# Layer norm with gelu, bound by DMA: 2 MB transfers of 16 KB runs, and the result written over the input's buffer

## Chip, cores, metric

One core of a Trainium2 chip. The metric is the device time of one execution in microseconds (us), median of several. "The profile" is the page and the views made from the trace of one profiled execution, whose span leaves out about 1.8 us of the measured time.

## The reference

```python
mean = np.mean(x, axis=-1, keepdims=True)          # x: 8 x 1024 x 2048 float32
var = np.var(x, axis=-1, keepdims=True)
out = gamma * (x - mean) / np.sqrt(var + eps) + beta
return 0.5 * out * (1 + np.tanh(np.sqrt(2 / np.pi) * (out + 0.044715 * out ** 3)))
```

It reads 67.1 MB and writes 67.1 MB.

## The kernel before

The 8192 rows are cut into 64 tiles of 128 rows, one row of 8 KB per partition. A tile is loaded (1 MB). DVE takes its statistics, ACT normalises it to bf16, DVE multiplies by gamma, and TensorE adds beta into PSUM. ACT then applies gelu from PSUM into an output buffer, which is stored (1 MB). Loads and stores are all issued by SP in one order.

```python
xin  = ctx.enter_context(tc.tile_pool(name="xin", bufs=AHEAD + 2))    # 12 buffers of 8 KB a partition
outs = ctx.enter_context(tc.tile_pool(name="outs", bufs=6))           # 6 buffers of 8 KB a partition
# gamma once and beta twice: 8 KB rows into single partitions, issued from ACT
def load(i):
    xt = xin.tile([P, d], f32, tag="xt")
    o(nc.sync.dma_start(out=xt, in_=xf[i * P:(i + 1) * P]))
def gelu(i):
    ot = outs.tile([P, d], f32, tag="ot")
    o(nc.scalar.activation(out=ot, in_=pss.pop(i), func=ACT.Gelu_apprx_tanh))
    o(nc.sync.dma_start(out=of[i * P:(i + 1) * P], in_=ot))
for t in range(T + 2):
    if t + AHEAD < T: load(t + AHEAD)          # AHEAD = 10
    if t < T: stats(t)
    if 0 <= t - 1 < T: norm(t - 1)
    if 0 <= t - 2 < T: gelu(t - 2)
    if 0 <= t - 1 < T: beta_mm(t - 1); scale(t - 1)
# ... (statistics, normalising and matmuls cut)
```

## Time and profile before

| what | value | how to read it |
|---|---|---|
| time | 325.39 us (325.36 to 325.52) | median |
| span of the profiled execution | 323.5 us | |
| DMA queue's share of 16 engines | 98.7% | the bound |
| busiest compute engine | ACT, 78% | has room |
| plateau | 426 GB/s from 36 to 310 us | |
| from 310 us to the end | 306 GB/s over 11.5 us | the only long stretch under the plateau |

The slices of the span, the stretches and the waits stand in the prediction.

### The profile page before, as it was taken

To read this page: it belongs to the slowest core of one execution; us is meant where nothing else is said; L and a number is where in the kernel's file an instruction comes from. 1 tells how busy PE (TensorE), PEld (TensorE's weight loads), DVE (VectorE), ACT (ScalarE), POOL (GpSimd) and SP (SyncE) were. 2 spreads that over 40 slices of the span, in tenths; PEclk is the share of its full clock that TensorE was granted. 3 is DMA by queue.
4 is the path that set the end of the run, shared out by engine and by line. 5 is a ranking of instruction groups with operands and counts; after the bars stand their busy time and mean duration, and the time that the engine had idled before them with its cause. 6 is when DMAs were issued, how large, how long until landed. Compare 5 with 4: busy or idle time off the path is not lost.

```text
span 323.5 us, 2348 instructions
## 1 busy us (share of the span) xinstructions
PE 239.9 (74%) x510; PEld 62.1 (19%) x520; DVE 249.9 (77%) x386; ACT 253.2 (78%) x132; POOL 123.7 (38%) x201
## 2 busy tenths in 40 slices
PE   5588888887776876866866867767768677686880
PEld 2122222222111111111211211111112111121220
DVE  3799999998787787787787887877877868778940
ACT  3779999987787877877877877878778777788982
POOL 1143444444435334344344244353353432524420
DMA  7999999999999999999999999999999999999976
GB/s 293 428 423 421 402 424 425 424 426 428 425 427 427 425 425 428 424 429 426 425 428 425 426 427 427 427 424 426 427 425 428 423 428 427 423 428 425 426 312 264
DMA packets 18452, 134.40 MB, mean 415 GB/s; under 512 B 2051, under 2 KB 2051, under 8 KB 2051
## 3 DMA queue, kind: packets, MB, share of 16 engines
q1 hardware_dynamic: 18432, 134.23, 98.7%
q8 instruction: 4, 0.07, 0.1%
q14 instruction: 10, 0.08, 0.1%
q10 hardware_dynamic: 6, 0.02, 0.0%
HBM read 67.13 MB, written 67.11 MB: 415 GB/s over the span
## 4 chain that ended last, share of the span: by engine, by line
issue 52%; POOL 37%; ACT 3%; DVE 3%; DMA 2%; another core or an unknown queue 0%; POOLq 0%; ACTq 0%
POOL nm L103 20%; POOL rs L101 11%; POOL ve L98 6%; DMA b_row<-in_beta_dram 2%; DVE st L94 2%; ACT ot L130 1%; DVE b_hl L139 1%; ACT yk L110 1%; ACT b_hi L81 1%; ACT b_hl L80 1%; DVE zg L122 0%; POOLq L101 0%; DVE mv L96 0%; ACT L46 0%
## 5 line engine op out<-in xcount | busy, mean ns | idle before, releaser
L126 PE MATMUL ps<-zg,ident 128*128 128x512 bf16 x246 | 116.1, 620 | 68.1 <-DVE zg L122 63.9
L94 DVE BATCH_NORM_STATS2 st<-xt 128x6 f32<-128x512 f32 x256 | 157.7, 678 | 4.2 <-DMA xt<-in_x_dram 4.2
L130 ACT ACTIVATE ot<-ps 128x2048 f32<-128x2048 f32 x64 | 119.9, 1873 | 51.2 <-DMA out_dram<-ot 49.8
L110 ACT ACTIVATE yk<-xt,nm,rs 128x2048 bf16<-128x2048 f32 x64 | 133.4, 2084 | 8.0 <-POOL nm L103 8.0
L117 PE MATMUL ps<-b_hl,ones_b 33*128 33x512 bf16 x256 | 120.5, 624 | 4.2 <-DVE b_hl L139 2.1
L122 DVE TENSOR_TENSOR zg<-yk,g_t 128x2048 bf16<-128x2048 bf16 x64 | 78.0, 1218 | 51.2 <-ACT yk L110 51.2
L98 POOL TENSOR_SCALAR ve<-mv 128x1 f32<-128x1 f32 x64 | 19.8, 309 | 175.0 <-DVE mv L96 175.0
L103 POOL TENSOR_SCALAR nm<-mv,rs 128x1 f32<-128x1 f32 x64 | 66.8, 1044 | 6.3
L126 PEld LDWEIGHTS <-ident 128*128 128x128 bf16 x256 | 32.4, 127 | 153.9 <-issue 153.1
L117 PEld LDWEIGHTS <-ones_b 33*128 33x128 bf16 x256 | 27.1, 127 | 92.6 <-issue 91.1
L101 POOL TENSOR_TENSOR rs<-ve,mhalf 128x1 f32<-128x1 f32 x64 | 36.1, 564 | 5.3
L96 DVE BATCH_NORM_AGGREGATE mv<-st 128x2 f32<-128x24 f32 x64 | 16.9, 264 | 6.3
L86 PE MATMUL g_ps<-g_row,ones 1*128 1x512 f32 x8 | 7.2, 1072 | 3.7 <-DMA g_row<-in_gamma_dram 3.7
L80 ACT ACTIVATE b_hl<-b_row 1x2048 bf16<-1x2048 f32 x1 | 1.9, 1908 | 4.8 <-DMA b_row<-in_beta_dram 4.8
L86 PEld LDWEIGHTS g_ps<-g_row,ones 1*128 1x128 f32 x8 | 2.5, 325 | 6.8 <-issue 6.8
L139 DVE TENSOR_TENSOR b_hl<-b_row,b_hi 1x2048 bf16<-1x2048 f32 x1 | 2.3, 2280 | 1.8 <-ACT b_hi L81 1.8
L88 ACT ACTIVATE g_t<-g_ps 128x2048 bf16<-128x2048 f32 x1 | 1.9, 1877 | 0.3 <-PE g_ps L86 0.3
L81 ACT ACTIVATE b_hi<-b_row 1x2048 bf16<-1x2048 f32 x1 | 1.9, 1908 | 0.0
L46 ACT ACT_TABLE_LOAD x1 | 1.3, 1283 | 0.7 <-PEq L163 0.7
L78 DVE MEMSET b_hl<- 33x1024 uint32 x1 | 0.9, 912 | 1.0 <-PEq L163 1.0
L73 POOL TENSOR_SCALAR_AFFINE_SELECT ident<-ident 128x128 bf16<-128x128 bf16 x1 | 0.3, 293 | 0.1
L66 POOL MEMSET ones<- 1x128 f32 x1 | 0.2, 194 | 0.3 <-POOLq L163 0.3
(7 smaller groups left out, 0.9 us busy)
## 6 DMA issues: line engine op xcount, KB each, us to landing
xt<-in_x_dram SPq DMA_DIRECT2D x64, 1024.0 KB, 19.5
out_dram<-ot SPq DMA_DIRECT2D x64, 1024.0 KB, 19.6
b_row<-in_beta_dram ACTq DMA_DIRECT2D x2, 8.0 KB
g_row<-in_gamma_dram ACTq DMA_DIRECT2D x1, 8.0 KB
```

The source lines that it names most:

```text
L86: o(nc.tensor.matmul(g_ps[:, c], lhsT=ones, rhs=g_row[:, c], start=True, stop=True))
L94: o(nc.vector.bn_stats(out=st[:, j, :], in_=xr[:, j, :]))
L96: o(nc.vector.bn_aggr(out=mv, in_=st))
L98: o(nc.gpsimd.tensor_scalar(out=ve, in0=mv[:, 1:2], scalar1=float(eps), scalar2=1.0, op0=ALU.add, op1=ALU.mult))
L101: o(nc.gpsimd.tensor_tensor(out=rs, in0=ve, in1=mhalf, op=ALU.pow))
L103: o(nc.gpsimd.tensor_scalar(out=nm, in0=mv[:, 0:1], scalar1=rs, scalar2=-1.0, op0=ALU.mult, op1=ALU.mult))
L110: o(nc.scalar.activation(out=yk, in_=xts.pop(i), func=ACT.Identity, scale=rs, bias=nm))
L117: o(nc.tensor.matmul(ps[:, c], lhsT=ones_b, rhs=b_hl[:, c], start=True, stop=False))
L122: o(nc.vector.tensor_tensor(out=zg, in0=yks.pop(i), in1=g_t, op=ALU.mult))
L126: o(nc.tensor.matmul(ps[:, c], lhsT=ident, rhs=zg[:, c], start=False, stop=True))
L130: o(nc.scalar.activation(out=ot, in_=pss.pop(i), func=ACT.Gelu_apprx_tanh))
L139: o(nc.vector.tensor_tensor(out=b_hl[32:33], in0=b_row[32:33], in1=b_hi[32:33], op=ALU.subtract))
```

## The change

Its intent is longer runs and fewer transfers: a partition holds two consecutive rows, so that a transfer has 2 MB in runs of 16 KB. It also drops the separate output buffers: gelu writes over x, and ten buffers of 16 KB serve loads and stores.

```diff
+R = 2
+SLOTS = 10
+AHEAD = 8
+    xg = xf.rearrange("(b p r) d -> b p r d", p=P, r=R)
+    og = of.rearrange("(b p r) d -> b p r d", p=P, r=R)
-    xin = ctx.enter_context(tc.tile_pool(name="xin", bufs=AHEAD + 2))
-    outs = ctx.enter_context(tc.tile_pool(name="outs", bufs=6))
+    big = ctx.enter_context(tc.tile_pool(name="big", bufs=SLOTS))
+    def load(b, pieces):
+        xt = big.tile([P, R, d], f32, tag="xt")
+        k = R // pieces
+        for q in range(pieces):
+            o(nc.sync.dma_start(out=xt[:, q * k:(q + 1) * k], in_=xg[b, :, q * k:(q + 1) * k]))
+        xts[b] = xt
 ...
-        ot = outs.tile([P, d], f32, tag="ot")
-        o(nc.scalar.activation(out=ot, in_=pss.pop(i), func=ACT.Gelu_apprx_tanh))
-        o(nc.sync.dma_start(out=of[i * P:(i + 1) * P], in_=ot))
+        o(nc.scalar.activation(out=xts[i // R][:, i % R], in_=pss.pop(i), func=ACT.Gelu_apprx_tanh))
 ...
-        if t + AHEAD < T:
-            load(t + AHEAD)
+            if (t - 2) % R == R - 1:
+                b = (t - 2) // R
+                store(b, R if b == B - 1 else 1)
+                if b + AHEAD < B:
+                    load(b + AHEAD, 1)
```

The cuts hold the store (the mirror of the load), the rows of gamma and beta in one buffer, and a smaller rearrangement of the beta rows. The first pair is loaded, and the last one stored, in two pieces of 1 MB.

## The prediction

> **What bounds the kernel now.** I read the page's busy shares first. The busiest compute engine is ACT at 78%, so no compute engine is the bound. The slices of the span and the queue table come next:
>
> ```profile
> DMA  7999999999999999999999999999999999999976
> DMA packets 18452, 134.40 MB, mean 415 GB/s; under 512 B 2051, under 2 KB 2051, under 8 KB 2051
> q1 hardware_dynamic: 18432, 134.23, 98.7%
> ```
>
> The 16 DMA engines are full in 37 of 40 slices. Nearly all bytes are x in (67.1 MB) and the result out (67.1 MB), so a floor of bytes divided by rate sets the time. The page's chain of the work that ended last calls half the span "issue" and walks through small POOL lines; it does not show this bound, so I leave it aside. Next I cut the span into stretches (start:end, length, five busy times, TensorE clock, DMA share, GB/s):
>
> ```profile
> 0.00:3.00 3.00, 0.00 (x0) 0.00 (x0) 0.91 (x1) 1.28 (x1) 0.99 (x9) 1.00 0.30 76
> 3.00:32.00 29.00, 22.62 (x42) 6.55 (x43) 22.79 (x35) 21.35 (x12) 7.87 (x15) 1.00 1.01 424
> 32.00:36.00 4.00, 3.85 (x10) 1.02 (x9) 3.86 (x7) 3.36 (x2) 1.84 (x3) 1.00 0.95 377
> 36.00:310.00 274.00, 208.34 (x451) 53.21 (x459) 221.09 (x343) 221.11 (x116) 112.16 (x172) 1.00 1.01 426
> 310.00:321.50 11.50, 5.07 (x11) 1.28 (x11) 1.23 (x1) 6.06 (x4) 0.81 (x2) 1.00 0.74 306
> 321.50:323.50 2.00, 0.00 (x0) 0.00 (x0) 0.00 (x0) 0.00 (x0) 0.00 (x0) 1.00 0.01 4
> ```
>
> The last number is what to see. There is a start of 3 us, a long plateau at 424 to 426 GB/s, a short dip around 34 us where the first stores follow the first loads, then **11.5 us at only 306 GB/s**, then 2 us for the last write to be confirmed. The tail is the one place where DMA waits for compute. The waits and the queue's own order say why:
>
> ```profile
> ACT ot L130 <- DMA out_dram<-ot: 49.8, 46, 1.9
> SPq L59 <- DMA xt<-in_x_dram: 113.0, 55, 3.5
> SPq L131 <- ACT ot L130: 36.9, 12, 4.6
> ...
> 272.80 45.70 SPq L131 DMA_DIRECT2D out_dram<-ot  x13
> ```
>
> The gelu waits 49.8 us for one of six output buffers to be stored, so compute can never be more than six stores ahead of DMA. When the loads end (last load issued at 270.3 us, 19.5 us to landing, so about 290), a store needs about 2.46 us of DMA, but ACT needs 2.08 + 1.87 = 3.95 us per tile. The backlog of at most six stores runs out at about 310 us, and the last stores come at compute's pace, each waited for by the queue. The last gelu ends at 318.2 us, then a whole 1 MB store follows.
>
> ```profile
> xt<-in_x_dram SPq DMA_DIRECT2D x64, 1024.0 KB, 19.5
> out_dram<-ot SPq DMA_DIRECT2D x64, 1024.0 KB, 19.6
> ```
>
> A landing time of 19.5 us is eight transfers of 2.45 us. The built program shows eight completion semaphores used in turn, so a transfer is issued when the eighth before it has landed. The queue is deep and its waits (113 us) cost nothing.
>
> **What the Trainium skill says.** (1) "DMA: Bandwidth & Descriptors", section "Where 436 GB/s comes from": 16 ports x 32 B x 850 MHz give a ceiling of 435.2 GB/s. The trace's plateau, 426, is 2.1% under it. So the whole steady part has at most 2.1% to give. (2) Same page, "The descriptor swizzle": a 1 MiB transfer is 8 data descriptors and one completion descriptor per engine. The trace agrees exactly: 128 transfers x 16 engines x 9 = 18432 packets, and 128 x 16 = 2048 of the 2051 small ones are completions. (3) Same page, "Why small descriptors are slow": about 3 bus cycles of fixed overhead per packet. My estimate from it: 8 KB is 256 beats of 32 B, 3 more are 1.2%; that would explain over half of the 2.1% and leave the rest to the completion. The trace gives no duration of one packet, so this is not confirmed. (4) "SBUF — State Buffer", section "The DMA setup-cost knee": about 2 us fixed per transfer, so larger transfers are faster. The trace does not support counting that here: with eight transfers in flight it sits beside other transfers' data, and 1 MB transfers already run at 426 GB/s. It appears once, as the 2 us at the end.
>
> **The change, part by part.**
>
> Compute is nearly untouched: the same 64 tiles pass through the same instructions, one b_hi buffer goes, and the bias matmuls keep their place in PE's order. ACT still writes 128x2048 f32 into SBUF. I count 0 us here.
>
> *Part 1, larger runs and half as many transfers.* At 426 GB/s 1 MB takes 2.461 us; at 435.2 it would take 2.409. The gap is 52 ns per transfer, shared by 8 descriptors and a completion. A 2 MB transfer with 16 KB runs has again 8 descriptors and one completion per engine. If the whole gap is a fixed cost of these, 26 ns per MB go, times 128 MB = **3.3 us**. If the gap comes with the bytes[...], nothing goes. The load-only stretch (424) is not faster than the mixed one (426) with the same descriptors, which says that part of the gap belongs to memory and not to the descriptors. I take half: **1.6 us**.
>
> *Part 2, the result overwrites x.* The wait of gelu for an output buffer disappears, as its place is the input tile already there. Compute's own pace shows before that wait starts to bite: one pair of tiles about every 8.3 us (statistics groups at 12.9, 21.2, 29.5 us in the chain). DMA needs 4 x 2.46 = 9.84 us per pair for load and store together. So compute gains about 1.5 us per pair on DMA and would finish its last pair by about 25 + 31 x 8.3 = 282 us, or, if it catches up with the loads, some 12 us after the last load lands. The last load is issued after 24 store-load rounds; about 56 of the 64 transfer slots of 2 MB precede its landing, so about 2.5 + 56 x 4.92 = 278 us, and the last gelu ends at about 290. By then eight pairs of stores, some 39 us of DMA work, are waiting or just issued: the tail is filled. The stretch from 310 us on moved 306 x 11.5 = 3.52 MB, which at 426 takes 8.26 us: **3.2 us** go.
>
> *Part 3, ten buffers for both directions.* The load of pair b+8 needs the store of pair b-2 landed. In issue order that store is followed by load b+6, store b-1, load b+7 and store b, four transfers or 19.7 us of queued work, as much as now. The program's waits of the queue confirm it: a steady load waits for the store four places back. So no bubble is expected. At the start, 8 loads are 16 MB or 39 us, while the first store is ready at about 25 us (two tiles instead of one, first store now at 21.7): no bubble either. The first pair is loaded in two 1 MB pieces, so compute starts as now.
>
> Sum: the start 3 us; 134.40 - 0.23 = 134.17 MB at 426 are 315.0 us; the dip costs 0.5; the end 2.0: 320.4 us of span with part 2 alone. Less 1.6 is 318.8. The time on the clock is about 1.85 us over the span (325.32 against 323.5), so about **320.6**, that is 1.5% faster.
>
> **Rivals.** *A, the tail only:* bytes cost what they cost, part 1 gives nothing: 320.4 + 1.85 = 322.3. For it: the load-only rate, and that the skill's ceiling may not be reachable from HBM. Against: the packet arithmetic of place (3) fits the gap. *B, all fixed cost:* 317.1 + 1.85 = 319.0, just short of 2% (the line is 318.9). Only a lost dip or a rate beyond the ceiling's proportion would pass it. *C, a wait takes the place of the one removed:* one buffer now serves load, compute and store, and the queue is one in-order list, so a store that waits for the second tile of its pair blocks the load behind it. Each such bubble would show as GB/s under 420 in the plateau, and ten of 1 us would eat the gain: 325 to 330. For it: the queue already waits 36.9 us for gelu. Against: those waits lie at the start and in the tail, and by the numbers above the queued work leads by some 17 us at store 3 and more later. *D, engines drift apart:* with 2 MB transfers the slowest of 16 engines ends later and the tail fades out; perhaps 1 us back, 321.5.
>
> **Range and chances.** A and B span 319.0 to 322.3; I widen this to 318.3 below (lost dip, slightly better rate) and 322.8 above (D or a small bubble on A). Faster by over 2% needs all of B and a bit: 0.18. Slower by over 2% needs C in full: 0.03. The rest, 0.79, within 2%.
>
> **What would show each step right or wrong.** Packets on the first queue should fall to 66 x 16 x 9 = 9504; near 17400 would mean that 16 KB runs are cut, and part 1 void. The plateau's rate decides part 1: 426 is A, 429 my half, 431 B. For part 2 the gelu's wait for the store must be gone from the waits, the last gelu must end well before 310 us, and the rate after 310 us must stay above 420 until 2 us before the end. Part 3 is wrong if a slice in the middle falls under 420, or if the queue's waits for ACT are long after the start. The prediction fails upward if the plateau runs below 424 with 16 KB runs, downward if it runs above 432.

## More of the kernel before

A point to keep in mind for later: "DMA share" and GB/s are means over 16 engines. One engine alone is 426 / 16 = 26.6 GB/s, or a share of 0.06.

## The result, and the profile after

The changed kernel took 322.38 us (321.12 to 322.57) against 325.39 us. The ratio is 0.9899, with a 95% interval of 0.9873 to 0.9924: 1% faster, "same" at the 2% line. The profiled execution was the fastest of the four (321.12 us, span 319.4). The unaltered kernel was timed twice more below: 321.26 and 321.86 us.

The queue's lines of the page after:

```profile
DMA packets 9523, 134.39 MB, mean 421 GB/s; under 512 B 1059, under 2 KB 1059, under 8 KB 1059
q1 hardware_dynamic: 9504, 134.22, 98.8%
xt<-in_x_dram SPq DMA_DIRECT2D x31, 2048.0 KB, 24.3
out_dram<-xt SPq DMA_DIRECT2D x31, 2048.0 KB, 28.7
```

Exactly 9504 packets: the 16 KB runs are not cut. ACT's waits after:

```profile
ACT yk L121 <- POOL nm L114: 37.7, 32, 2.9
ACT b_hl L91 <- DMA rows<-in_beta_dram: 4.5, 1, 4.5
ACT xt L137 <- issue: 1.5, 1, 1.5
```

The 49.8 us of waiting for an output buffer are gone. ACT now waits for its statistics, which in the end wait for loads. The stretches after, in the columns that the prediction explains:

```profile
3.00:32.00 29.00, 22.84 (x43) 6.68 (x44) 23.01 (x36) 21.57 (x12) 7.90 (x15) 1.00 1.00 428
36.00:310.00 274.00, 216.12 (x470) 54.24 (x468) 219.65 (x344) 224.34 (x119) 98.47 (x174) 1.00 1.01 429
310.00:314.00 4.00, 0.00 (x0) 0.00 (x0) 0.00 (x0) 0.00 (x0) 0.00 (x0) 1.00 0.99 418
314.00:316.00 2.00, 0.00 (x0) 0.00 (x0) 0.00 (x0) 0.00 (x0) 0.00 (x0) 1.00 0.69 291
316.00:318.00 2.00, 0.00 (x0) 0.00 (x0) 0.00 (x0) 0.00 (x0) 0.00 (x0) 1.00 0.21 90
```

Three things are to be seen. The plateau rose from 426 to 429 GB/s. Compute is done long before the end: from 310 us on no engine computes (the last gelu started at 293.5 us), so the tail is not set by compute any more. And still the rate fades, from 418 over 291 to 90 GB/s, although every store was issued by 296 us. The four microseconds from 314 to 318 moved 2 x 291 + 2 x 90 = 762 KB of the 1716 KB that 429 GB/s would have moved, so about 2.2 us of full rate are missing.

**Engine by engine.** The trace lists every DMA packet's start, duration, size and queue, but not its engine. Packets of one engine follow each other with an overlap of 3 to 4 ns, eight of data and then one completion, so they can be joined into 16 chains. Some joins are doubtful, most of them in kernels of 8 KB runs. The ends of the chains do not depend on them: a second joining by other rules gave the same 16 ends. Which engine carried which packets long before the end does depend on them, and is not shown. What came out:

```
changed kernel, end of each of the 16 engines' data (us):
314.5 314.7 314.7 314.8 315.0 315.2 315.2 315.5 315.7 315.8 316.3 316.6 317.5 317.7 317.8 318.0
steady distance from one packet's start to the next: 8 KB 306 ns, 16 KB 607 ns, completion 5 to 6 ns
```

The fade is 16 engines with equal bytes finishing at different times, 3.5 us apart. The same lateness was in the kernel before, hidden in its tail. Stretches of the kernel before, cut finer:

```profile
315.05:315.35 0.30, 0.30 (x2) 0.15 (x1) 0.00 (x0) 0.00 (x0) 0.00 (x0) 1.00 0.07 27
315.50:318.00 2.50, 0.31 (x1) 0.00 (x0) 0.00 (x0) 1.73 (x1) 0.00 (x0) 1.00 1.00 413
318.40:318.90 0.50, 0.00 (x0) 0.00 (x0) 0.00 (x0) 0.00 (x0) 0.00 (x0) 1.00 0.04 16
319.00:321.50 2.50, 0.00 (x0) 0.00 (x0) 0.00 (x0) 0.00 (x0) 0.00 (x0) 1.00 1.01 416
```

In the first and third stretch about one engine's share is left (0.07 and 0.04 against 1/16 = 0.06; a packet is counted where it starts). From 1.65 to 321.99 us there is no moment in the trace at which no packet is in progress. At the two narrow places one packet at a time is, on one late engine. That engine worked through both bubbles that the other 15 spent waiting for compute.

At the very end it was only a little behind the others, though. The last store has one completion packet per engine: 15 of them came between 321.51 and 321.67 us, because the last gelu started only at 316.27 us, and the late engine's at 321.99 us. So the kernel before had two limits, compute's last store and the late engine, and they lay only 0.3 us apart.

So two theories stood after the result:

- **Theory T** (the prediction's own): the bubble in the tail was lost time, and filling it gains 3.2 us. Something else then gave back part of the gain.
- **Theory E**: the end is set by the one DMA engine that comes last. The tail's bubble was idleness of engines that had time to spare, so filling it gains next to nothing, and only work taken off every engine counts.

### The profile page after: what moved, and what is told of

Same layout as the page of the kernel before. It is cut to its first block, busy times and chain, and to the rows that moved or that the text cites. A ratio compares the mean times of both kernels' runs of the same rounds, so it can differ in the third digit from the quotient of the medians.

```text
span 319.4 us, 2219 instructions
## 1 busy us (share of the span) xinstructions
PE 242.8 (76%) x520; PEld 61.9 (19%) x520; DVE 247.2 (77%) x386; ACT 250.5 (78%) x132; POOL 109.4 (34%) x201
## 3 DMA queue, kind: packets, MB, share of 16 engines
q1 hardware_dynamic: 9504, 134.22, 98.8%
## 4 chain that ended last, share of the span: by engine, by line
issue 35%; POOL 29%; ACT 14%; DVE 7%; PE 5%; DMA 2%; POOLq 0%; ACTq 0%
POOL ve L109 12%; POOL rs L112 9%; POOL nm L114 8%; ACT yk L121 7%; PE ps L133 5%; ACT xt L137 5%; DVE zg L130 4%; DMA rows<-in_beta_dram 2%; DVE st L105 2%; DVE b_hl L143 1%; ACT b_hl L92 1%; ACT b_hl L91 1%; POOLq L112 0%; DVE mv L107 0%; ACT L65 0%
## 5 line engine op out<-in xcount | busy, mean ns | idle before, releaser
L133 PE MATMUL ps<-zg,ident 128*128 128x512 bf16 x256 | 119.4, 620 | 45.0 <-DVE zg L130 40.1
L137 ACT ACTIVATE xt<-ps 128x2048 f32<-128x2048 f32 x64 | 119.0, 1860 | 1.5 <-issue 1.5
L109 POOL TENSOR_SCALAR ve<-mv 128x1 f32<-128x1 f32 x64 | 39.2, 613 | 166.3 <-DVE mv L107 132.9
L130 DVE TENSOR_TENSOR zg<-yk,g_t 128x2048 bf16<-128x2048 bf16 x64 | 76.4, 1193 | 16.9 <-ACT yk L121 16.9
L112 POOL TENSOR_TENSOR rs<-ve,mhalf 128x1 f32<-128x1 f32 x64 | 35.2, 550 | 5.3
L114 POOL TENSOR_SCALAR nm<-mv,rs 128x1 f32<-128x1 f32 x64 | 34.0, 531 | 6.3
L97 PE MATMUL g_ps<-rows,ones 1*128 1x512 f32 x8 | 7.2, 1072 | 3.6 <-DMA rows<-in_gamma_dram 3.6
L91 ACT ACTIVATE b_hl<-rows 1x2048 bf16<-1x2048 f32 x1 | 1.9, 1909 | 4.5 <-DMA rows<-in_beta_dram 4.5
L97 PEld LDWEIGHTS g_ps<-rows,ones 1*128 1x128 f32 x8 | 2.5, 325 | 6.7 <-issue 6.7
L143 DVE TENSOR_TENSOR b_hl<-rows,b_hl 1x2048 bf16<-1x2048 f32 x1 | 2.3, 2282 | 1.7 <-ACT b_hl L92 1.7
L92 ACT ACTIVATE b_hl<-rows 1x2048 bf16<-1x2048 f32 x1 | 1.9, 1910 | 0.0
```

The lines of the kernel that those rows point to most:

```text
L97: o(nc.tensor.matmul(g_ps[:, c], lhsT=ones[64:65], rhs=rows[64:65, c], start=True, stop=True))
L109: o(nc.gpsimd.tensor_scalar(out=ve, in0=mv[:, 1:2], scalar1=float(eps), scalar2=1.0, op0=ALU.add, op1=ALU.mult))
L112: o(nc.gpsimd.tensor_tensor(out=rs, in0=ve, in1=mhalf, op=ALU.pow))
L114: o(nc.gpsimd.tensor_scalar(out=nm, in0=mv[:, 0:1], scalar1=rs, scalar2=-1.0, op0=ALU.mult, op1=ALU.mult))
L130: o(nc.vector.tensor_tensor(out=zg, in0=yks.pop(i), in1=g_t, op=ALU.mult))
L133: o(nc.tensor.matmul(ps[:, c], lhsT=ident, rhs=zg[:, c], start=False, stop=True))
```

## The experiments

All of them gave correct results. Each was timed in up to five rounds, beside the kernel before on the same chip (325.40 or 325.44 us in those jobs). The changed kernel itself, unaltered, took 322.38 us in the first result, 321.26 us beside e4 to e6 (run e8) and 321.86 us on the chip of all the others (run e12). A difference to it is therefore uncertain by about half a microsecond, and I give it against the nearest repeat too.

### e1: the in-place part alone, 1 MB transfers of 8 KB runs

```diff
-R = 2
-SLOTS = 10
-AHEAD = 8
+R = 1
+SLOTS = 20
+AHEAD = 16
```

> The changed kernel with one row per partition: 1 MB transfers of 8 KB runs as in the kernel before, but the result still overwrites x, 20 buffers of 8 KB, 16 loads ahead. Parts 2 and 3 of the change alone. Theory T (the prediction's part 2: filling the tail saves 3.2 us by itself): 322.2 us. Theory E (the end is set by the one DMA engine with the most work, which in the kernel before never idles from 1.65 to 321.99 us, so the tail bubble was idleness of the other 15): no gain, 325.0 to 325.7 us, and in the profile the DMA share fades out over some 4 us at the end.

Measured: 325.05 us against 325.44, ratio 0.9988 (0.9976 to 1.0000). Stretches of this run:

```profile
308.00:316.00 8.00, 0.00 (x0) 0.00 (x0) 0.00 (x0) 0.00 (x0) 0.00 (x0) 1.00 1.01 426
316.00:318.00 2.00, 0.00 (x0) 0.00 (x0) 0.00 (x0) 0.00 (x0) 0.00 (x0) 1.00 0.81 340
318.00:320.00 2.00, 0.00 (x0) 0.00 (x0) 0.00 (x0) 0.00 (x0) 0.00 (x0) 1.00 0.19 82
320.00:321.50 1.50, 0.00 (x0) 0.00 (x0) 0.00 (x0) 0.00 (x0) 0.00 (x0) 1.00 0.07 27
```

The tail is filled, 426 GB/s until 316 us, and it gained 0.4 us. The last 1.5 us are one engine alone at 27 GB/s. Theory T is refuted: the bubble is gone, and the fade at the end takes its place.

### e7: the larger runs alone, with separate buffers

```diff
-    big = ctx.enter_context(tc.tile_pool(name="big", bufs=SLOTS))
+    big = ctx.enter_context(tc.tile_pool(name="big", bufs=6))
+    outs = ctx.enter_context(tc.tile_pool(name="outs", bufs=3))
-        o(nc.scalar.activation(out=xts[i // R][:, i % R], in_=pss.pop(i), func=ACT.Gelu_apprx_tanh))
+        if i % R == 0:
+            ot = outs.tile([P, R, d], f32, tag="ot")
+            ots[i // R] = ot
+        o(nc.scalar.activation(out=ots[i // R][:, i % R], in_=pss.pop(i), func=ACT.Gelu_apprx_tanh))
 ... (AHEAD = 5, loads issued as soon as their buffer has been read)
```

> Part 1 alone: 2 MB transfers of 16 KB runs, but six separate pair buffers for x and three for the result as in the kernel before (same bytes of buffers), 5 pairs loaded ahead. Theory E: most of the gain is there, 322.4 to 323.5, as the bubbles of the tail fall on the engines with less work (unless they grow over the 3 us of lead that those engines have). Theory T: only the rate's gain, and the tail's loss stays or grows with the larger pieces: the profile's gain of 4.1 us less 3.2, so 324.4 or more.

Measured: 323.09 us (five runs of 322.49 to 323.24, one of 326.35), ratio 0.9941 (0.9912 to 0.9971). Its stretches:

```profile
300.00:308.00 8.00, 7.37 (x16) 1.86 (x16) 7.33 (x13) 7.36 (x5) 2.85 (x6) 1.00 0.78 330
308.00:312.00 4.00, 3.53 (x8) 0.82 (x7) 1.48 (x2) 4.00 (x3) 0.54 (x1) 1.00 0.63 266
```

Here the tail has bubbles over 12 us, worse than in the kernel before, and yet this kernel is only 0.7 us slower than the changed one in its first result (322.38), or 1.2 us against e12 (321.86). The large runs bring most of the gain without the filled tail, as theory E says. But here no late engine sets the end: at 309.1 us all engines were idle at once, for 0.7 us, so the late one had caught up, and the 16 completions of the last store came within 0.15 us (319.69 to 319.84). The end of e7 is that of compute's last store.

### e2: 2 MB transfers of 8 KB runs

```diff
-    xg = xf.rearrange("(b p r) d -> b p r d", p=P, r=R)
-    og = of.rearrange("(b p r) d -> b p r d", p=P, r=R)
+    xg = xf.rearrange("(b r p) d -> b p r d", p=P, r=R)
+    og = of.rearrange("(b r p) d -> b p r d", p=P, r=R)
```

> The changed kernel with the two rows of a partition 128 rows apart, so the transfer has still 2 MB but is made of 8 KB runs. Packets on the first queue about 2*31*16*17 + 4*16*9 = 17440. If the cost goes with the run (packet): as the 1 MB in-place kernel, less 64 completions of about 6 ns, 0.4 us: about 325. If it goes with the transfer: as the changed kernel, 322.4.

Measured: 323.43 us, ratio 0.9944 (0.9931 to 0.9957), with 17440 packets as expected. It lies between the two answers. Between e1 (325.05) and the changed kernel lie 2.7 us (3.2 against e12): 1.6 come with the larger transfer and 1.1 (1.6 against e12) with the longer run. The packets' arithmetic gave the transfer only 0.4. My expectation of about 325 was wrong. The ends of the engines, listed under e3, say where the 1.6 us lie: the first engine to finish ends only 0.3 us earlier than in e1, as the arithmetic says, but the last one 1.1 us earlier. So it is not a cost that each transfer has on every engine; with fewer transfers the last engine was less late.

### e13: the change of direction as the cause of that

```diff
-            if (t - 2) % R == R - 1:
-                b = (t - 2) // R
-                store(b, R if b == B - 1 else 1)
-                if b + AHEAD < B:
-                    load(b + AHEAD, 1)
+            if (t - 2) % 2 == 1:
+                for b in (t - 3, t - 2):
+                    store(b, 1)
+                for b in (t - 3, t - 2):
+                    if b + AHEAD < B:
+                        load(b + AHEAD, 1)
```

> The in-place kernel with 1 MB transfers of 8 KB runs (e1, 325.05), but with two stores and then two loads in the queue's order, so the queue changes direction as often as with 2 MB transfers. Run e2 (2 MB of 8 KB runs, 323.43) was 1.6 us faster than e1, of which the 64 completions fewer explain 0.4. If the change of direction costs the rest: 323.8. If it is the number of transfers itself: 325.

Measured: 325.23 us, ratio 0.9993 (0.9979 to 1.0008), as e1. Changing direction half as often brings nothing. What remains is the number of transfers, or something that goes with it; why the last engine is less late with fewer of them is open.

### e3: 4 MB transfers of 32 KB runs

```diff
-R = 2
-SLOTS = 10
-AHEAD = 8
+R = 4
+SLOTS = 5
+AHEAD = 4
```

> The changed kernel with 4 rows per partition: 4 MB transfers of 32 KB runs, 5 buffers of 32 KB, 4 loads ahead. If a packet has a fixed cost (two 8 KB packets follow each other every 306 ns, two 16 KB ones every 607, so about 5 ns per packet), an engine has half as many again: about 256 x 5 ns = 1.3 us less than the changed kernel, 321.0 us. If the gain of 16 KB runs has another cause (alternation of loads and stores, tail): 322.4; if the coarser pieces open bubbles: 324 or more.

Measured: 321.71 us (320.98 to 322.34), ratio 0.9886 (0.9873 to 0.9899). That is the changed kernel's own ratio when it was repeated (0.9888, e12), so no gain is shown. The chains tell why:

```
end of data (us):            first engine   last engine
e1   1 MB, 8 KB runs         316.8          321.3
e2   2 MB, 8 KB runs         316.5          320.2
changed, 16 KB runs          314.5          318.0
e3   4 MB, 32 KB runs        313.3          317.9
steady step of a 32 KB packet: 1209 ns
```

On the engine that finishes first the packets' arithmetic holds. Two packets of 8 KB less one of 16 KB are 2 x 306 - 607 = 5 ns, and two of 16 KB less one of 32 KB are 2 x 607 - 1209 = 5 ns. The changed kernel has 496 packets of 16 KB per engine in place of 992 of 8 KB: 2.5 us expected, 2.0 seen from e2. The 240 packets of 32 KB of e3 should save 1.2 us, and 1.2 were seen. The last engine followed for the step to 16 KB (320.2 to 318.0, in single profiled executions), but hardly for the step to 32 KB (318.0 to 317.9). It seems to have had more slow packets instead, but that rests on doubtful joins.

### e4, e5: one engine is given more work, and the control

```diff
+                if b == 12:
+                    o(nc.sync.dma_start(out=rows[1:18], in_=xf[0:17]))      # e4: 17 rows
+                    o(nc.sync.dma_start(out=rows[1:17], in_=xf[0:16]))      # e5: 16 rows
```

> The changed kernel plus one more load, issued after pair 12: 17 rows of x of 8 KB each into partitions that nothing reads. 17 partitions are not split, so all 139 KB should fall on the same engine as the gamma and beta rows. Theory E: that engine is the last to finish, so the time grows by 17 x 0.306 = 5.2 us, to about 327.6. If the mean rate of 16 engines counts: 0.3 us more, 322.7.

> The control: the same extra load with 16 rows in place of 17, which is split over 16 engines, one row each. Both theories: 0.3 us more than the changed kernel, 322.7.

Measured: 327.11 us (ratio 1.0052) with 17 rows, 322.89 us (0.9926) with 16 rows, in the same rounds. One more row of 8 KB, but all on one engine, costs 4.2 us more than 16 rows spread. The queue's lines show that the edits did what they should: 18 packets more than the changed kernel's 9504 in e4 (17 rows and one completion, so one engine) and 32 more in e5 (16 rows and 16 completions):

```profile
q1 hardware_dynamic: 9522, 134.36, 97.3%
q1 hardware_dynamic: 9536, 134.35, 98.5%
```

The profile of e4 shows the engine alone at the end:

```profile
318.00:320.00 2.00, 0.00 (x0) 0.00 (x0) 0.00 (x0) 0.00 (x0) 0.00 (x0) 1.00 0.11 45
320.00:323.50 3.50, 0.00 (x0) 0.00 (x0) 0.00 (x0) 0.00 (x0) 0.00 (x0) 1.00 0.06 26
```

The share of 0.06 at 26 GB/s is one engine of 16. The 4.2 us are less than the 17 x 0.306 = 5.2 us of the rows; the engine that got them need not be the one that would have been last. Against the repeat e8 in the same rounds (321.26 us), the 17 rows cost 5.9 us, and the 16 spread ones 1.6 us where both theories expected 0.3. The control agreed with its 322.7 only because that was reckoned from 322.38; why one more small load costs so much is open.

### e6: the same load in the kernel before

```diff
+    extra = singles.tile([17, d], f32)
+            if t - 2 == 25:
+                o(nc.sync.dma_start(out=extra[0:17], in_=xf[0:17]))
```

> The kernel before with the same load of 17 rows after tile 25. Theory E: its busiest engine never idles, so 5.2 us more: 330.6. Theory T: the tail is set by compute, which has 3 us of bubbles there to hide a late engine: at most 2 us more, 327.5.

Measured: 329.22 us (four runs of 329.2 to 329.6, two of 327.2 and 327.5), ratio 1.0101: 3.8 us more than 325.40. That is nearer to theory E's 5.2 than to the at most 2 expected from theory T. But the two theories are not told apart as cleanly as I had meant. The last gelu before, and in e6:

```profile
316.27 1.88 ACT L130 ACTIVATE ot<-ps 128x2048 f32<-128x2048 f32 x1 [1.45 <-remote]
320.50 1.88 ACT L131 ACTIVATE ot<-ps 128x2048 f32<-128x2048 f32 x1 [1.45 <-remote]
```

Compute's own tail moved by 4.2 us, which theory T's "at most 2" had left out. The last gelu that waited for an output buffer started at 292.71 us before and at 296.92 us in e6: the extra rows lay on one engine alone, so a buffer seems to come free only when the last engine has done its part of the store. All 16 engines then ended together (325.76 to 325.92 us). So the kernel before does wait for one late engine, but in e6 by way of its output buffers and of compute.

### e8, e12: the changed kernel repeated

e8 was meant to spread the gamma and beta rows over 16 engines.

```diff
-    o(nc.scalar.dma_start(out=rows[64:65], in_=gamma[None, :]))
-    ...
+    for p, v in ((64, gamma), (0, beta), (32, beta)):
+        o(nc.scalar.dma_start(out=rows[p:p + 1].rearrange("p (a f) -> p a f", a=16), in_=v.rearrange("(o a f) -> o a f", o=1, a=16)))
```

> The changed kernel with the three rows of gamma and beta loaded as 16 pieces of 512 B each, so that no engine gets three whole rows. Theory E: the engine that ended last (317.97 us) loses about 0.9 us of work, but the next ones ended at 317.81 and 317.72, having fetched instructions; so 0.2 us less in the end, up to 0.9 if those vary: 321.5 to 322.3, and the fade at the end a bit steeper. If the rows do not matter: 322.4.

Measured: 321.26 us, ratio 0.9880 (0.9867 to 0.9893). The experiment failed: the pieces are contiguous, were joined again, and the page shows the same 6 packets on that queue. It counts as a repeat. e12 is a true one, the kernel without any edit:

> The changed kernel once more, unaltered, to see how far its time varies from one job to the next on a chip: 321.2 to 322.6 as in the record and in e8.

Measured: 321.86 us (321.36 to 321.97), ratio 0.9888 (0.9876 to 0.9901). With the first result the change is worth 1.0 to 1.2%. The changed kernel varies by more than 1 us between executions (321.1 to 322.6), the kernel before by only some 0.4.

### e10, e11: the rows really spread

By my joining of the changed kernel's profile, the engine that carried the three rows (3 x 0.31 us) was the last.

```diff
-    rows = singles.tile([65, d], f32)
+    rows = singles.tile([65, 16, d // 16 + 16], f32)      # a gap after every 128 values
+    rv = lambda p, a=0, b=16: rows[p:p + 1, a:b, 0:d // 16]
-    o(nc.scalar.dma_start(out=rows[64:65], in_=gamma[None, :]))
+    o(nc.scalar.dma_start(out=rv(64), in_=v3(gamma)))     # v3: 1 x 16 x 128 view
 ... (beta alike, readers adapted; e11 also R = 4, SLOTS = 5, AHEAD = 4)
```

> The run e8 built the same three whole-row transfers as the changed kernel (contiguous pieces were joined again; 6 packets on their queue as before), so it was a repeat of it. Here the rows' buffer has a gap after every 128 values, so each row is really 16 pieces of 512 B (3 x 16 x 2 = 96 packets on that queue). Theory E: the engine that carried the rows loses about 0.95 us of work, and it ended last in the changed kernel's profile, next ones 0.2 us before it: 0.2 to 0.9 us less than the changed kernel in the same rounds. If the rows do not matter: the same.

> The same with 4 rows per partition (4 MB transfers of 32 KB runs). In the profile of 4 rows, the engine with the rows ended last at 317.8 and the fastest at 313.3. Theory E: rows off that engine, and 5 ns less per 32 KB on all: 1 us less than the changed kernel, 320.5 to 321.3, the best of all. Otherwise 321.7 as with 4 rows alone.

Measured, in the rounds of e12 (321.86): e10 322.44 us (ratio 0.9912), e11 322.08 us (0.9901). Neither is better. The queue of e10 shows the edit worked this time:

```profile
q10 hardware_dynamic: 96, 0.02, 0.0%
```

And still one engine came last, at 319.2 us in the chains, while the first ended at 314.5. The rows are not what makes an engine late. By the chains that engine carried three of the 13 packets with which the core fetches instructions, and had slow packets beside, but which engine carried those is not shown, as the joins far from the end are doubtful. What makes one engine late by 3 to 5 us is left open. The durations give a hint that needs no joining: in the changed kernel 71 packets took over 100 ns longer than usual, 21 of them in the first 5 us and 28 between 30 and 60 us, around the first stores. All packets together took 32 us longer than at their usual durations, 2.0 us per engine, which is of the size of the lateness.

## Why the prediction was right or wrong

The time (322.38, against 320.6 predicted, 318.3 to 322.8) lay in the range, and "same" was the likeliest outcome. But the sum was partly right by luck: of 4.8 us of forecast gain, 3.2 came from a term that measured 0.4, and 1.6 from one that measured 2.7 to 3.2. The errors had opposite signs. Rival A's 322.3 is the measured time, by luck alone: its one term was the wrong one.

**What bounds the kernel: right, but one step short.** DMA is the bound. I read its mean of 16 engines as one machine. The step that failed is "The tail is the one place where DMA waits for compute": 15 of its engines did, the late one that ends 0.3 us after them did not.

**Part 1, 1.6 us: right in kind, too small.** The gain from packets and transfers is the difference between e1 and the changed kernel, 325.05 - 322.38 = 2.7 us (3.2 with e12's 321.86), near rival B's 3.3 and not the half that I took. The plateau of 429 GB/s matched my half by the mark that I had set. The fixed cost per packet measured 5 ns. I had said that the trace gives no duration of one packet; it does, and I could have measured this beforehand (one step of 306 ns at 8 KB). My split of the 52 ns gap between descriptors and completion did not foresee that with fewer transfers the last engine is also less late (e2: 1.6 us in place of 0.4). The objection about the load-only stretch did not hold: that stretch rose as well, from 424 to 428 GB/s.

**Part 2, 3.2 us: the wrong step.** What it said of compute was right: the output wait disappeared, the last gelu ended at 295.4 us (I had "about 290"), and compute left the tail. "3.2 us go" failed: e1 put it at 0.4 us. Compute's last store and the late engine were two limits 0.3 us apart, and the change took only the first away. The sign I had set for it failed too: after 310 us the rate was 418 GB/s and not above 420, and it faded from 314 us, long before the last 2 us.

**Part 3, no bubbles: right.** From slice 7 on no slice but the last is under 426 GB/s. The dip at the first stores moved from 34 to about 42 us (387 GB/s from 40 to 44; it makes slice 6, at 401). One of my signs against this part did appear: the queue waited for ACT long after the start, 28.5 us from 260 us on. It cost nothing there, as the stores already issued kept the rate at 429 GB/s and more until 306 us.

**The rivals.** A is refuted (part 1 gave most of the gain). C did not come. D was the right rival, named but underrated: "engines drift apart ... perhaps 1 us back". The fade took 2.2 us of mean rate, and I had not seen that the same drift already lay under the tail of the kernel before, nor that it does not come with the 2 MB transfers: e1, with 1 MB, ends 4.5 us apart. The sign of it was there to be read in the trace of the kernel before: a share of about 0.06 at 315.05 and 318.40 us.

## What to carry to other kernels

Where DMA is the bound, 16 engines with equal bytes need not finish together (3.5 us apart here). The end is then the later of two: the last engine's, and that of compute's last store. Before filling a bubble in the tail, look whether the rate in it goes to zero or only down to one engine's share. If one engine never stops, filling the bubble removes one limit and leaves the other (0.4 us gained here, of 3.2 hoped for). Then expect gain from what every engine is spared, above all packets, and not from the bubble. Look for loads that fall on one engine, since 17 rows cost 4.2 us more here than 16.

## What the Trainium skill lacked or had wrong

- "DMA: Bandwidth & Descriptors", section "Why small descriptors are slow": about 3 cycles per packet, at 850 MHz an estimate of 3.5 ns. The runs show about 5 ns per packet at 8, 16 and 32 KB (steps of 306, 607 and 1209 ns), so the page's kind of cost is confirmed with a slightly larger figure, of which the 32 bytes of descriptor metadata that the same section adds may be a part (not shown here). It still counts at 8 KB: the longer run was worth 1.1 to 1.6 us of 323.4.
- "SBUF — State Buffer", section "The DMA setup-cost knee": with a full queue its 2 us per transfer do not show. Half as many transfers with the same runs saved 1.6 us over the whole kernel, and only 0.3 us on the engine that finishes first. No page has a figure for a full queue.
- No page I used puts a number on how far apart the 16 engines of one stream finish: 3.5 us in the changed kernel, 4.5 us in e1, with equal bytes. "DMA: Bandwidth & Descriptors" has remarks without a figure: a bulk load runs at the pace of its slowest engine, and engines 7 and 15 are usually slower. The trace does not number the engines, so whether the late ones are these is not shown.
- The same page, section "Why a DMA increments its semaphore by 16 and not by 1", says how many engines a transfer uses; by it a partition count with no divisor from 2 to 16 goes to one engine. Confirmed by e4, whose 17 rows added one completion packet (16 rows: 16) and which ended with one engine at 26 GB/s; the time it costs at the end of a kernel (4.2 us for 17 rows) is not on the page.
